# A mixture-of-experts stage on one Trainium2 core: fetching an expert's rows two experts ahead, with six-column one-hot products

## The chip, the cores and the metric

The kernel runs on one core of one Trainium2 chip. The metric is device time in microseconds (us) of one execution, lower is better. PE is the matrix engine TensorE, PEld its weight loads, DVE the VectorE, ACT the ScalarE, POOL the GpSimd engine, which issues indirect DMAs (gathers and scatters), and SP the engine that issues the weight loads from HBM. SBUF is the on-chip memory, PSUM the accumulator that PE writes.

## What is computed

The reference is one layer of a diffusion backbone for 512 tokens of width 1024: modulation from a conditioning vector, a mixer (RWKV-7 heads beside Fourier heads), a gated residual with layer norm, a second modulation, then a mixture of 32 experts and a last gated residual with layer norm. The part that matters here is the mixture:

- A router picks for each token 4 of 32 experts and gives softmax gates over the four.
- An expert is `y = W2 · swiglu(W1 · x + b1) + b2` with W1 of 1024 x 2048 and W2 of 1024 x 1024 in float32; `swiglu(g, l) = min(g, 7) · sigmoid(1.702 · min(g, 7)) · (clip(l, -7, 7) + 1)`.
- A token's result is the sum over its four experts of gate times y.

All 32 experts' weights, 12 MB each, are read once.

## The kernel before

The mixer and the router take the first part of the span; the expert stage begins at about 705 us, and a last layer norm closes the kernel.

**Capacities.** The experts are sorted by load and each place in a fixed list `PLAN` has a capacity of 32 to 192 rows, taken up as blocks of 64 or 32 rows: 53 blocks for the 32 places e0 to e31. (A loop for experts that overflow their capacity is in the program, and isn't executed.)

**Fetch.** `Expert.fetch` finds the tokens of an expert and gathers their rows. For a block, `slots` compares each token's rank in the expert with a row of numbers (one DVE instruction, `O`, a one-hot matrix of 512 tokens x 128 slots in bf16) and multiplies it on PE with a narrow right side `R6`: three columns give the row's index in parts (`onehot`, line 1249, 16 matmuls in 128 x 32 tiles, four of them side by side in the array). DVE makes the index `idx` of it (lines 1265 to 1269), and POOL issues the gather `xg` (line 1303). A second `onehot` over three other columns gives the gates, summed on DVE into `gt` (line 1275), which is needed only when the expert's result is scaled.

**Split, up, turn, down, put.** `split` transposes the gathered rows on PE (line 1314) and ACT copies them to `xt` (1316). `up` multiplies by W1 in 8 slices; each slice is one DMA of 1 MB into a `raw` tile (line 1326, on SP), used by the matmuls `st<-raw,xt` (line 1335) of every block, with the bias added at the end (1342) and swiglu on DVE and ACT (1369 to 1373). `turn` transposes the activations (1387, copy `at` on ACT 1389). `down` multiplies by W2 in four 1 MB tiles (`st<-raw,at`, also line 1335) and DVE scales by the gate into `y` (1406). `put` adds `y` to the rows of `accd` in HBM by an accumulating scatter (POOL, line 1412); these scatters follow one another, each waits for the landing of the one before. Four products `b2_part` (1477, `yb` 1478) add the gated b2 in the early experts.

**Order.** `all_experts` writes the stage as: for expert i, fetch of i+1, up of i, turn of i-1, split of i+1, down of i-1, put of i-1. The 384 weight loads go round 14 `raw` buffers, in program order on SP. [...] Buffers: two PSUM tiles `pt` for one-hot products and transposes, six for `st`; four gathered blocks `xg64` and two `xg32`; three `sel` (a column that adds the right expert's bias).

Of the kernel before, what the change touches and what calls it, by code (L numbers as in the profile page):

```python
# [1136 lines left out]
def _plan():  # L1137

    of = {n: [j for j in range(1, NE) if CAPS[j] == n] for n in (32, 64, 96)}
    plan = [0, of[32].pop()]  # L1140
    for j, rest in zip((3, 1, 4, 2, 5, 6), ((32, 96, 64, 96), (32, 64, 96, 64), (32, 96, 64, 96), (32, 64, 96, 64),
                                            (32, 96, 64, 96), (64, 96, 64, 32))):
        plan += [j] + [of[n].pop() for n in rest]
    return [(j, CAPS[j]) for j in plan]


PLAN = _plan()


def blocks(cap):  # L1150

    return [(o, min(64, cap - o)) for o in range(0, cap, 64)]
# [35 lines left out]
def moe(tc, I, ck, h2d, accd, modd, P):  # L1188
# [56 lines left out]
    def onehot(p, O, rhs, c):  # L1245
        for j in range(4):
            for i in range(4):
                q = slice(32 * i, 32 * i + 32)
                PE.matmul(p[q, c], O[:, j, q], rhs[:, j, c], start=(j == 0), stop=(j == 3), tile_position=(0, 32 * i))  # L1249

    def slots(cap, r, rhs):


        res = []
        ps = pst.tile([128, 512], F32, name="pt", tag="pt")
        for o, n in blocks(cap):
            w = 128 // n
            O = B.tile([128, 4, 128], BF16, "O", 5)
            io = M["iota"][:, o:o + n].unsqueeze(1).unsqueeze(1).to_broadcast([128, 4, w, n])
            V.tensor_tensor(O.rearrange("p j (a s) -> p j a s", s=n), io,  # L1260
                            r.unsqueeze(2).unsqueeze(2).to_broadcast([128, 4, w, n]), op=ALU.is_equal)
            p = ps[:, o // 8:o // 8 + 6]
            onehot(p, O, rhs, slice(0, 3))
            s3 = B.tile([128, 3], F32, "s3", 6)
            V.tensor_copy(s3, p[:, 0:3])  # L1265
            V.scalar_tensor_tensor(s3[:, 0:1], s3[:, 2:3], M[f"trash{n}"], s3[:, 0:1], op0=ALU.mult, op1=ALU.add)
            V.tensor_tensor(s3[:, 0:1], s3[:, 0:1], s3[:, 1:2], op=ALU.add)
            idx = B.tile([128, 1], I32, "idx", 10)
            V.tensor_scalar(idx, s3[:, 0:1], float(w), M[f"base{n}"], op0=ALU.mult, op1=ALU.add)  # L1269
            gt = B.tile([128, 1], F32, "gt", 10)  # L1270
            res.append((idx, gt, O, p))
        yield [z[0:2] for z in res]
        for _, gt, O, p in res:
            onehot(p, O, rhs, slice(3, 6))
            V.tensor_reduce(gt, p[:, 3:6], mybir.AxisListType.X, ALU.add)

    def part(i, n):
# [3 lines left out]
    class Expert:  # L1281
# [10 lines left out]
            return self  # L1292

        def fetch(self):
            more = slots(self.cap, self.r, self.rhs)
            self.sl = next(more)
            sel = B.tile([96, 64], BF16, "sel", 3)
            G.tensor_copy(sel, self.selcol.to_broadcast([96, 64]))  # L1298
            self.sel.append(sel)
            self.xs = []  # L1300
            for (idx, _), n in zip(self.sl, self.bl):
                x = B.tile([128, 8 * n], F32, f"xg{n}", n // 16)
                G.indirect_dma_start(out=x, out_offset=None, in_=h2h[n],  # L1303
                                     in_offset=bass.IndirectOffsetOnAxis(ap=idx[:, 0:1], axis=0))
                self.xs.append(x)
            for _ in more:
                pass
# [156 lines left out]
    def place(i):  # L1464
        j, cap = PLAN[i]
        return Expert(cap, rm[:, :, j], R6[:, :, j], sel3[:, j:j + 1])

    def chosen(i):
        j = PLAN[i][0]
        return SY.value_load(eidi[0:1, j:j + 1], min_val=0, max_val=NE - 1)  # L1470

    def b2_part(j):

        y = B.tile([128, D], F32, "yb", 1)
        for n in range(2):
            p = pst.tile([128, 512], F32, name="pt", tag="pt")
            PE.matmul(p, gwT[:, j * 128:(j + 1) * 128], b2r[:, n * 512:(n + 1) * 512], start=True, stop=True)
            A.activation(y[:, n * 512:(n + 1) * 512], p, AF.Copy)
        G.indirect_dma_start(out=accd[:, :], out_offset=bass.IndirectOffsetOnAxis(ap=toki[:, j:j + 1], axis=0),
                             in_=y, in_offset=None, compute_op=ALU.add)  # L1480

    def all_experts():
        cur, prev = first, None
        yield cur.split
        for i in range(len(PLAN)):
            nxt = place(i + 1) if i + 1 < len(PLAN) else None
            if nxt:
                yield nxt.fetch
            ups = list(cur.up())
            yield from ups[:8 if nxt else 4]  # L1490
            if nxt:
                nxt.weights(chosen(i + 1))
            if prev:
                yield prev.turn
            if nxt:
                yield nxt.split
            if prev:
                yield from prev.down()
                yield prev.put
                if 4 <= i < 8:  # L1500
                    yield lambda j=i - 4: b2_part(j)
            if not nxt:
                yield from ups[4:]
            prev, cur = cur, nxt
        yield prev.turn
        yield from prev.down()
        yield prev.put
# [14 lines left out]
    B = Buffers(None, 99, (praw, RAWA))  # L1522
    first = Expert(PLAN[0][1], rm0, R60, M["sel0"][0:96]).weights(0)
    experts = Run(all_experts())
    experts.load(RAWA)
    sb_ = ExitStack()
# [24 lines left out]
    for j in P.order:  # L1551
        tk = slice(j * 128, (j + 1) * 128)
        p = mixer(j)
# [200 lines left out]
    with ExitStack() as sv:  # L1754
# [3 lines left out]
        with tc.For_i(0, nov, 1) as k:  # L1758
# [8 lines left out]
            r, gq = pv.tile([128, 4], F32, name="ovr"), pv.tile([128, 4], F32, name="ovg")  # L1767
# [3 lines left out]
            rhs = pv.tile([128, 4, 6], BF16, name="ovrhs")  # L1771
# [68 lines left out]
```

## Time and profile before

| | before |
|---|---|
| median of 3 runs | 1832.53 us (1828.89 to 1835.13) |
| the profiled execution: its own time / span | 1826.18 us / 1824.4 us |
| mean granted TensorE clock, as a share of full speed | 0.934 |
| PE busy | 1627.3 us (89%) |
| PE weight loads busy | 890.5 us (49%) |
| DVE busy | 766.7 us (42%) |
| ACT busy | 390.4 us (21%) |
| POOL busy | 433.0 us (24%) |
| DMA | 572.83 MB, mean 314 GB/s |

The span is what the profiler records of one execution from its first to its last instruction; the run's own time is 1.8 us more. A row of a timeline gives start, length, engine, line and shapes (a float32 matmul instruction leaves two records in it); brackets at its end give the time that the engine sat idle just before, and what ended it. `SPq` is SP's own queue, and a wait of it for PE at line 1326 is a weight load that waits for a `raw` buffer to come free.

### The profile page before, as it was taken

What the parts mean: (1) busy time and instruction counts of PE and PEld (TensorE: products, weight loads), DVE (VectorE), ACT (ScalarE), POOL (GpSimd) and SP (SyncE); (2) the same over time, 40 slices, a digit from 0 to 9 for tenths busy, and PEclk for the clock granted to TensorE, in tenths of its full rate; (3) what the DMA queues carried; (4) which work ended last, traced back from release to release, by engine and by line L of the source; (5) the groups of instructions that cost most, each with busy time, mean ns of one, the idle gap of its engine ahead of it and who ended that gap; (6) DMA issues with size and microseconds to landing.
All of it is one profiled execution on the core that took longest, in us unless ns stands there. A gap on an engine that the chain in (4) does not pass through costs nothing. (4 is left out here: it accounts for less than half of the span.)

```text
span 1824.4 us, 40583 instructions
## 1 busy us (share of the span) xinstructions
PE 1627.3 (89%) x16964; PEld 890.5 (49%) x16964; DVE 766.7 (42%) x1775; ACT 390.4 (21%) x767; POOL 433.0 (24%) x436
## 2 busy tenths in 40 slices
PE   4889887686999977999989999999999999999980
PEld 1767655566787763454334443444344344434430
DVE  4899967878446673221122121222022221212113
ACT  3565455232224250100011000100010100001001
POOL 1543444264134351111120211011011110111113
PEclk9899988786899977999999999999999999999995
DMA  8568759574675638989997999999999999999993
GB/s 318 173 202 258 243 186 280 167 219 142 179 238 186 211 128 332 379 317 408 403 395 248 390 407 405 415 406 415 396 351 404 411 407 409 412 409 410 404 385 113
DMA packets 205514, 572.83 MB, mean 314 GB/s; under 512 B 28448, under 2 KB 116128, under 8 KB 156176
## 3 DMA queue, kind: packets, MB, share of 16 engines
q1 hardware_dynamic: 144912, 521.16, 73.9%
q0 software_dynamic: 11840, 24.91, 5.9%
q10 hardware_dynamic: 48576, 24.12, 4.7%
q8 instruction: 136, 2.23, 0.5%
q14 instruction: 50, 0.41, 0.1%
HBM read 512.57 MB, written 57.56 MB: 313 GB/s over the span
## 5 line engine op out<-in xcount | busy, mean ns | idle before, releaser
L1335 PE MATMUL st<-raw,xt 128*32 128x512 f32 (+1 forms) x6784 | 644.7, 521 | 5.9 <-ACT xt L1316 5.2
L1335 PEld LDWEIGHTS st<-raw,xt 128*32 128x32 f32 x6784 | 249.4, 109 | 329.4 <-issue 269.1
L1335 PE MATMUL st<-raw,at 128*32 128x512 f32 (+1 forms) x3392 | 324.4, 521 | 10.5 <-ACT at L1389 7.6
L1335 PEld LDWEIGHTS st<-raw,at 128*32 128x32 f32 x3392 | 115.2, 110 | 190.8 <-issue 148.4
L1369 DVE TENSOR_SCALAR sg<-st 128x256 f32<-128x256 f32 x87 | 36.4, 418 | 366.3 <-PE st L1342 366.3
L1370 ACT ACTIVATE sth<-sg 128x256 f32<-128x256 f32 x87 | 35.9, 415 | 572.2 <-DVE sg L1369 572.1
L1412 POOL DMA_INDIRECT accd<-y,idx x53 | 84.7, 1597 | 247.5 <-DVE y L1406 119.9
L1406 DVE SCALAR_TENSOR_TENSOR y<-st,gt,gt2h 128x512 f32<-128x512 f32 (+1 forms) x53 | 34.6, 654 | 236.8 <-PE st L1335 214.6
L1303 POOL DMA_INDIRECT xg<-h2d,idx x53 | 54.2, 1022 | 316.1 <-DVE idx L1269 295.8
L328 PE MATMUL pj<-hhi,wl 128*128 128x512 f32 (+1 forms) x240 | 89.9, 376 | 9.6 <-DVE wl L324 9.6
L328 PE MATMUL pj<-hhi,wh 128*128 128x512 f32 (+1 forms) x240 | 88.7, 372 | 9.8 <-DVE hlo L281 9.8
L1298 POOL CAST sel<-sel 96x64 bf16<-96x64 f32 x31 | 7.8, 254 | 361.6 <-PE st L1342 356.2
L328 PE MATMUL pj<-hlo,wh 128*128 128x512 f32 (+1 forms) x240 | 89.7, 374 | 0.0
L1316 ACT ACTIVATE xt<-pt 128x512 f32<-128x512 f32 (+1 forms) x53 | 27.3, 518 | 268.8 <-PE pt L1314 268.6
L652 PE MATMUL big<-Rb,Lt 128*128 128x256 f32 (+1 forms) x192 | 53.3, 428 | 14.9 <-DVE pk L658 6.4
L1265 DVE COPY s<-pt 128x3 f32<-128x3 f32 x53 | 8.3, 156 | 133.2 <-PE pt L1249 133.2
L1249 PEld LDWEIGHTS <-O 128*32 128x32 bf16 x1696 | 38.4, 95 | 51.6 <-issue 43.2
L328 PEld LDWEIGHTS pj<-hhi,wl 128*128 128x128 f32 x240 | 46.8, 195 | 21.6 <-DVE wl L324 12.4
L328 PEld LDWEIGHTS pj<-hhi,wh 128*128 128x128 f32 x240 | 46.8, 195 | 19.2 <-DVE hlo L281 10.1
L1389 ACT ACTIVATE at<-pt 128x512 f32<-128x512 f32 (+1 forms) x53 | 26.5, 517 | 132.1 <-PE pt L1387 131.8
L752 POOL TENSOR_TENSOR SW<-S,Wc 64x128 f32<-64x128 f32 (+1 forms) x66 | 31.3, 474 | 96.2 <-DVE S L787 77.5
L407 DVE SCALAR_TENSOR_TENSOR acc<-war,sil,acc 128x512 f32<-128x512 f32 x56 | 52.8, 943 | 0.8 <-ACT acc L404 0.6
(389 smaller groups left out, 2342.7 us busy)
## 6 DMA issues: line engine op xcount, KB each, us to landing
raw<-in_w SPq DMA_DIRECT2D x384, 1024.0 KB, 17.0
war<-in_w_ada SPq DMA_DIRECT2D x64, 256.0 KB, 3.3
chd<-pk ACTq DMA_DIRECT2D x52, 256.0 KB, 5.3
wr<-in_w_in ACTq DMA_DIRECT2D x40, 256.0 KB, 5.7
wa<-in_w_ada SPq DMA_DIRECT2D x16, 512.0 KB, 8.0
win<-chd SPq DMA_DIRECT2D x8, 896.0 KB, 5.6
win<-chd SPq DMA_DIRECT2D x16, 448.0 KB, 3.4
ltd<-Lt SPq DMA_DIRECT2D x8, 768.0 KB, 6.2
```

Of the source, the lines that this page charges most:

```text
L328: PE.matmul(p, a[:, k, :], b[:, k0 + k, t0:t0 + n], start=(k0 + k == 0 and i == 0), stop=(k0 + k == KD - 1 and i == 2))
L407: V.scalar_tensor_tensor(acc, wr, sil0[:, k:k + 1], acc, op0=ALU.mult, op1=ALU.add)
L652: PE.matmul(ps[:, z], Lu[:, u0 + (z0 + z if d == 0 else 3 - z0 - z), :], Rb[:, z0 + z], start=True, stop=True)
L752: G.tensor_tensor(SW[HALF[p]].rearrange("p z d c -> p (z d) c"), S[HALF[p], :, :, p].rearrange("p z d c -> p (z d) c"), Wc[HALF[p], 2 * c0 ...
L1249: PE.matmul(p[q, c], O[:, j, q], rhs[:, j, c], start=(j == 0), stop=(j == 3), tile_position=(0, 32 * i))
L1303: G.indirect_dma_start(out=x, out_offset=None, in_=h2h[n], in_offset=bass.IndirectOffsetOnAxis(ap=idx[:, 0:1], axis=0))
L1316: A.activation(xt.rearrange("p k s -> p (k s)"), p, AF.Copy)
L1335: PE.matmul(r, x(s * slices + b, o), c(raw[:, b * 2048 // slices:(b + 1) * 2048 // slices]), start=(s + b == 0 and first), stop=(s == n - ...
L1369: V.tensor_scalar(g, u2[:, :, 0], 7.0, None, op0=ALU.min)
L1370: A.activation(t, g, AF.Tanh, scale=0.851)
L1406: V.scalar_tensor_tensor(y, st, gt, gt2h[n], op0=ALU.mult, op1=ALU.mult)
L1412: G.indirect_dma_start(out=acch[n], out_offset=bass.IndirectOffsetOnAxis(ap=idx[:, 0:1], axis=0), in_=y, in_offset=None, compute_op=ALU.add)
```

## The change

It has two parts. `slots` gets an argument `once`: for every expert but the first, one group of 16 one-hot matmuls per block computes six columns, index and gates, instead of a group of three columns for the index and later one of three for the gates. And `all_experts` calls fetch two experts ahead: before up of i it fetches i+2 (and i=1 before the loop), where it fetched i+1.

```diff
-    def slots(cap, r, rhs):
+    def slots(cap, r, rhs, once):
...
-            onehot(p, O, rhs, slice(0, 3))
+            onehot(p, O, rhs, slice(0, 6 if once else 3))
...
         for _, gt, O, p in res:
-            onehot(p, O, rhs, slice(3, 6))
+            if not once:
+                onehot(p, O, rhs, slice(3, 6))
             V.tensor_reduce(gt, p[:, 3:6], mybir.AxisListType.X, ALU.add)
...
-            more = slots(self.cap, self.r, self.rhs)
+            more = slots(self.cap, self.r, self.rhs, self is not first)
...
         cur, prev = first, None
+        ahead = [place(i) for i in range(1, len(PLAN))]
         yield cur.split
+        yield ahead[0].fetch
         for i in range(len(PLAN)):
-            nxt = place(i + 1) if i + 1 < len(PLAN) else None
-            if nxt:
-                yield nxt.fetch
+            nxt = ahead[i] if i + 1 < len(PLAN) else None
+            if i + 2 < len(PLAN):
+                yield ahead[i + 1].fetch
```

Lines below it move by one or two: 1335 becomes 1337, 1303 becomes 1305, 1412 becomes 1414. Since the scheduler orders the instructions, the two programs were laid side by side, engine by engine. Over the expert stage 103 groups of 16 one-hot matmuls become 54, and 46 of them that stood at a place where the stream of `st` matmuls was not at a multiple of four become 17. Up to the bias of e17, the second expert with three blocks of 64 rows, 66 groups become 35, of which 30 and 12 are off that beat. Transposes `turn` that are followed directly by the `st` matmuls that need their copy go from 19 to 11 (up to there about half of them), and `split` so followed from 11 to 7. SP's order is the same in both.

On PE, at the block of 32 rows of an early expert (`R_5426` holds the columns, `at` belongs to the down pass that ends there, `xt` to the up pass that begins), the rows stand so; each LDWEIGHTS and MATMUL pair at line 1249 is repeated 16 times for a group. Before:

```order
L1335 MATMUL st<-raw,at_8054 32x256 x32
L1249 LDWEIGHTS O
L1249 MATMUL pt<-R_5426,O 32x3
...
L1335 MATMUL st<-raw,xt_8059 32x256 x19
L1249 LDWEIGHTS O
L1249 MATMUL pt<-R_5426,O 32x3
```

After:

```order
L1337 MATMUL st<-raw,at_8033 32x256 x32
L1249 LDWEIGHTS O
L1249 MATMUL pt<-R_5426,O 32x6
...
L1337 MATMUL st<-raw,xt_8038 32x256 x64
```

Before, groups of the fetch that ran beside this pass cut it after 19, 36 and 52 of its 64 matmuls; after, the 64 matmuls of the pass stand together.

On PE in the up pass of e17 (three blocks of 64 rows, `xt_12880`, `xt_12887`, `xt_12894` before and `xt_12431`, `xt_12438`, `xt_12445` after; `xg` with a transpose is the third block's split), eight matmuls per slice and block. Before:

```order
L1335 MATMUL st<-raw,xt_12880 32x512 x16
L1335 MATMUL st<-raw,xt_12887 32x512 x16
L1335 MATMUL st<-raw,xt_12880 32x512 x8
L1314 MATMUL pt<-mcst,xg_12616 128x128 x4
...
L1335 MATMUL st<-raw,xt_12894 32x512 x24
```

After (the first two blocks have gone through all eight slices by the rows ahead of these):

```order
L1337 MATMUL st<-raw,xt_12431 32x512 x8
L1337 MATMUL st<-raw,xt_12438 32x512 x8
...
L1344 MATMUL st<-b1s,sel 32x512
L1316 MATMUL pt<-mcst,xg_11963 128x128 x4
...
L1337 MATMUL st<-raw,xt_12445 32x512 x64
```

The third block's split moved from inside the pass to behind it, so its eight slices are used after the other two blocks are done with all of theirs.

On POOL at the end of the stage (each `accd` is a scatter, each `xg` a gather, `xg_17328` and `xg_16271` are those of the last expert). Before:

```order
L1412 DMA accd<-y_16322,idx 1280x512
L1303 DMA xg_17024<-h2d,idx 128x512
L1412 DMA accd<-y_16674,idx 1280x512
L1303 DMA xg_17328<-h2d,idx 128x256
L1412 DMA accd<-y_16676,idx 2560x256
L1412 DMA accd<-y_16988,idx 1280x512
L1412 DMA accd<-y_16990,idx 1280x512
L1412 DMA accd<-y_17295,idx 1280x512
L1412 DMA accd<-y_17544,idx 1280x512
L1412 DMA accd<-y_17546,idx 2560x256
L1412 DMA accd<-y_17627,idx 1280x512
L1412 DMA accd<-y_17717,idx 2560x256
```

After:

```order
L1414 DMA accd<-y_15981,idx 1280x512
L1305 DMA xg_16017<-h2d,idx 128x512
L1414 DMA accd<-y_15983,idx 2560x256
L1300 CAST sel<-sel_5427 96x64
L1414 DMA accd<-y_16235,idx 1280x512
L1305 DMA xg_16271<-h2d,idx 128x256
L1414 DMA accd<-y_16237,idx 1280x512
L1414 DMA accd<-y_16526,idx 1280x512
L1414 DMA accd<-y_16728,idx 1280x512
L1414 DMA accd<-y_16730,idx 2560x256
L1414 DMA accd<-y_16811,idx 1280x512
L1414 DMA accd<-y_16901,idx 2560x256
```

The last gather stands ahead of six scatters instead of eight, and its one-hot products stand one expert earlier on PE (in up of e29 instead of up of e30).

## Rows read from the trace of the kernel before

**Rows 1.** Windows of 20 us: time, busy time of each engine, clock, DMA.
```profile
core 0: us, PE busy (x) PEld busy (x) DVE busy (x) ACT busy (x) POOL busy (x), PEclk, DMA share, GB/s
920.00:940.00 20.00, 14.92 (x208) 6.33 (x206) 9.19 (x31) 3.90 (x8) 6.39 (x6) 0.91 1.03 401
...
980.00:1000.00 20.00, 19.53 (x211) 9.01 (x204) 9.04 (x26) 3.62 (x9) 0.26 (x2) 1.00 0.57 200
...
1300.00:1320.00 20.00, 20.00 (x192) 5.91 (x188) 0.00 (x0) 0.00 (x0) 1.57 (x1) 1.00 0.98 384
1320.00:1340.00 20.00, 19.53 (x266) 9.44 (x262) 9.98 (x30) 3.62 (x9) 3.89 (x4) 1.00 0.82 285
...
1420.00:1440.00 20.00, 20.00 (x252) 8.03 (x252) 5.01 (x19) 1.31 (x3) 4.77 (x5) 1.00 1.02 411
```

**Rows 2.** Waits of PE from 690 to 1800 us: total, times, longest.
```profile
PE st L1335 <- ACT at L1389: 7.6, 16, 0.7
PE st L1335 <- ACT xt L1316: 5.2, 10, 0.7
PE pt L1314 <- DMA xg<-h2d,idx: 4.6, 2, 3.7
...
PE st L1335 <- SPq L1758: 2.8, 2, 2.5
```

**Rows 3.** Waits of SP's queue from 800 to 1780 us.
```profile
SPq L1326 <- PE st L1335: 394.8, 195, 13.7
```

**Rows 4.** DMA issues of the page: count, size, median us from issue to landing.
```profile
raw<-in_w SPq DMA_DIRECT2D x384, 1024.0 KB, 17.0
```

**Rows 5.** Timeline of PE in up of e30: start, length, shapes, records.
```profile
1725.97 3.62 PE L1335 MATMUL st<-raw,xt 128*32 128x512 f32 x32
1729.41 0.26 PE L1249 MATMUL pt<-R,O 128*32 128x3 bf16 x16
1729.52 10.49 PE L1335 MATMUL st<-raw,xt 128*32 128x512 f32 x96
1739.82 0.62 PE L1342 MATMUL st<-b1s,sel 96*32 96x512 bf16 x8
```

**Rows 6.** Timeline of PE at a group that cuts the stream off the beat.
```profile
1222.19 3.18 PE L1335 MATMUL st<-raw,xt 128*32 128x512 f32 x27
...
1225.20 0.60 PE L1335 MATMUL st<-raw,xt 128*32 128x512 f32 x3
...
1225.68 0.60 PE L1335 MATMUL st<-raw,xt 128*32 128x512 f32 x1
...
1225.73 3.61 PE L1335 MATMUL st<-raw,xt 128*32 128x512 f32 x31
1229.12 0.26 PE L1249 MATMUL pt<-R,O 128*32 128x3 bf16 x11
```

**Rows 7.** Timeline of POOL's gathers and scatters at the end, some of them.
```profile
1727.91 0.99 POOL L1303 DMA_INDIRECT xg<-h2d,idx  x1 [28.97 <-DVE idx L1269]
1729.20 1.59 POOL L1412 DMA_INDIRECT accd<-y,idx  x1 [0.30 <-issue]
1738.90 1.57 POOL L1412 DMA_INDIRECT accd<-y,idx  x1 [8.11 <-DMA accd<-y,idx]
...
1791.11 1.55 POOL L1412 DMA_INDIRECT accd<-y,idx  x1 [3.74 <-issue]
```

**Rows 8.** Timeline of DVE, the scaled results of the last experts.
```profile
1726.12 0.75 DVE L1406 SCALAR_TENSOR_TENSOR y<-st,gt,gt2h 128x512 f32<-128x512 f32 x1 [4.64 <-PE pt L1249]
1752.01 1.34 DVE L1406 SCALAR_TENSOR_TENSOR y<-st,gt,gt2h 128x512 f32<-128x512 f32 x2 [8.71 <-PE st L1335]
1770.89 0.74 DVE L1406 SCALAR_TENSOR_TENSOR y<-st,gt,gt2h 128x512 f32<-128x512 f32 x1
1781.13 0.48 DVE L1406 SCALAR_TENSOR_TENSOR y<-st,gt,gt2h 128x256 f32<-128x256 f32 x1 [9.50 <-PE st L1335]
```

**Rows 9.** The chain that ended last, the piece behind the last scatter's issue.
```profile
1791.11 3.78 DMA accd<-y,idx
```

## The prediction

> **What bounds the kernel now.** I read the windows of 20 us first. In the expert stage PE is busy nearly all the time (19.5 to 20.0 of 20 us) at full clock, and at the same time the DMA engines are full: a share of 1.02 at 411 GB/s in the window at 1420 [rows 1], and so in nearly all windows of the stage. The places where transfers fall off are few: 200 GB/s at 980, 384 at 1300, 285 at 1320 [rows 1]; behind 1340 there is none up to 1760. So two limits lie side by side, and the list of waits has to say which ends last. PE waits little over 1100 us: 7.6 us in 16 waits for the copy `at`, 5.2 us in 10 for the copy `xt`, and 2.8 us for weights, nearly all of it once at the very end [rows 2]. SP's loads wait 394.8 us for PE to free a `raw` buffer [rows 3]. From this I take PE as the pace up to about 1340, with some weights landed ahead of it; from there the transfers run without a gap, the lead is used up, and at the end PE waits for the last tiles. What PE saves before 1340 can therefore move the end, and what it saves behind it cannot. After the weights comes a second chain: POOL's scatters, each behind the landing of the one before. The last `y` is ready at 1781.13 + 0.48 = 1781.6 [rows 8], yet its scatter is issued at 1791.11 [rows 7] and lands 3.78 us later [rows 9]; only then the layer norm starts. These 9.5 us are a queue on POOL.
>
> **The change part by part.**
>
> *One-hot groups.* A group that stands on the beat of the `st` stream: 96 records of 128 x 512 took from 1729.52 to 1739.82, 0.107 us each. The 32 records ahead of it need 3.43 us, and from 1725.97 to 1729.52 there are 3.55 [rows 5]: the group costs 0.12 us of PE. A group that cuts it: from 1222.19 to 1229.12 are 6.93 us with 62 `st` records, 6.65 us of work [rows 6], so 0.28 us; I take 0.30. The price of a group with six columns isn't in the trace. Three columns cost 0.12 us beside 512, so the weights and the issue rather than the columns set it; the bounds are 0.12 (columns free) and 0.24 (double), and I take 0.12, since a group's 0.12 us for 16 matmuls is next to one record of 512 columns (0.107). By the counts of the order, before the bias of e17 (at about 1325 us) 36 x 0.12 + 30 x 0.30 = 13.3 us become 23 x 0.12 + 12 x 0.30 = 6.4: -6.9 us. Behind it, 21 x 0.12 + 16 x 0.30 = 7.3 become 14 x 0.12 + 5 x 0.30 = 3.2: -4.1 us. With 0.24 for six columns, 23 x 0.12 and 14 x 0.12 come back, 2.8 and 1.7 us.
>
> The Trainium skill, "TensorE: Matmul & The Clock Gate", section "Back-to-back issue gap", gives matmuls of 1 to 64 columns one floor of about 25 ns each, whatever their width. That agrees with six columns costing as three; but 16 of them would be an estimated 0.40 us, where rows 5 show 0.12, since four of them stand side by side in the array. By the page the groups would be worth 49 x 0.40 = 19.6 us in all instead of 11.0; the row decides.
>
> *Waits on copies.* Where `turn` or `split` stands right before the product that needs its copy, PE waits 7.6 / 16 = 0.48 and 5.2 / 10 = 0.52 us [rows 2]. The order has 8 and 4 fewer such places: -3.8 - 2.1 = -5.9 us, about half of it, -3.0, before e17.
>
> So PE's own work is shorter by 6.9 + 3.0 = 9.9 us up to e17 and by 7.0 behind it. The 7.0 are hidden by the transfers, which have no gap there; without that cover they would count in full.
>
> *The third block of e17.* A new cost. Its eight `raw` tiles were freed one by one, each after three blocks. Now they are first freed after two blocks have gone through all eight: 128 instructions, 256 records of 0.107, 27.4 us in which none of eight of the 14 buffers comes free. What is under way then covers a load's median time from issue to landing, 17.0 us [rows 4]. So transfers rest for some 10.4 us. Before, there was a rest at the same place: (411 - 384) / 411 x 20 = 1.3 and (411 - 285) / 411 x 20 = 6.1 us [rows 1], 7.4 in all. The net is +3.0 us; bounds are +10.4 (the old rest was no part of it and stays) and 0. The second block of e27 is put off in the same way, by 13.7 us, less than the 17.0 under way: 0. All of this is late in being refilled, not in being used, so PE itself needn't wait there.
>
> PE's end: -9.9 + 3.0 = -6.9, taken as -7; bounds -17 (all of PE's saving counts, no new rest) and +0.5 (10.4 new, all of 9.9 saved).
>
> *The tail.* In up of e30, POOL waits 28.97 us for the last gather's index, while finished results stand behind it: the gather goes at 1727.91 and then eight scatters at steps of about 9.8 us (1729.20, 1738.90) [rows 7], though a `y` of them was ready long before. After, that gather stands one expert earlier, ahead of six scatters; its products stand in up of e29, which begins before 1700. Then the scatters can go as their `y` comes: 1726.9, 1752.8, 1762.6, 1772.4, and the last at 1782.2 by four steps of 9.8 from 1752.8 at the latest, next to 1781.6. In place of 1791.1 that is -9; bounds 0 and -9.5.
>
> *Others.* The same number of gathers, scatters, DVE index steps and loads is left; `gt` is now ready earlier, and its `tensor_reduce` is not on a path. Fetching earlier holds gathered rows and `idx` longer; PE waited for gathered rows only at the start of the stage, 4.6 us [rows 2], which the change doesn't touch (the first expert keeps its two groups). So the fetch itself buys nothing but the order.
>
> *Sum.* -7 - 9 = -16 us. The profiled execution's own 1826.2 becomes 1810.2; the median of before is 6.3 above it, and by the same difference I predict 1832.5 - 16 = **1816.5**.
>
> **The rivals.** About 0.3% (5.5 us) is what a measurement of this kernel can tell from no change.
>
> A, both terms as above: 1816.5, with its own range 1805 to 1820. Chance 0.45.
>
> B, the transfers bind before 1340 too, and PE's saving only makes it wait: for it speaks the full share in nearly every window [rows 1]; against it, that PE waits for no weights before the end [rows 2]. Then only the tail counts, and the e17 rest in part: -9, 1823.5. Chance 0.20.
>
> C, the tail is no shorter, because scatters pile up behind another gather or behind each other's landing; for it, that six steps of 9.8 us fill 59 of the last 90 us. PE's -7 is left: 1825.5. Chance 0.12.
>
> D, slower: the e17 hold hits when no tile is landed ahead. PE then stands for 10.4 us, and for some 2 more the clock is low, as in the window at 920, where 5 us of idle time went with a granted 0.91 over 20 us, below full speed for 0.09 x 20 = 1.8 us [rows 1]. With the transfers as the bound, PE's savings before it don't count, and PE comes to the tail that much later, with its scatters still in a row: +12.2 us, less the 7.4 of rest that transfers had at this place before if these were lost then too. That is 1837 to 1845. It decides from the point where PE shows a wait for `raw` of over 7 us between 1300 and 1345. Chance 0.10.
>
> The Trainium skill, same page, section "Loop structure matters more than you think", warns of just this: matmuls that wait for DMA run at the low clock afterwards. The window at 920, with 5 us idle and 0.91, agrees that idle time and a low clock come together here.
>
> E, no change that can be measured: one-hot products stood in PE's shadow of the weights anyway and the scheduler's order gives as it takes: 1832.5 within 5.5. For it, PE never waited for a gather but at the start. Chance 0.13.
>
> **How the numbers follow.** Faster is A, B and C: 0.77; the same 0.13, slower 0.10. The range reaches from 1804, a bit beyond A's bound with half of PE's hidden saving, to 1831, which takes in B and C and half of E, and leaves out D, the other half of E and some 0.04 below.
>
> **What would show it.** PE's line 1249 should fall to about half its instructions, the waits for `at` and `xt` to some 11 and 7 times. In the windows from 1300 to 1360 the transfers should dip deeper than before, with hardly a PE wait for `raw`. The last scatter should be issued within 1.5 us of the last `y`, and that `y` 7 us earlier than 1781.6. It is wrong if PE's idle time for `raw` moves from the end into the stage, if the last `y` is not earlier, or if scatters still stand in a row of 9.8 us steps up to the end.

## The result, and the profile after

The changed kernel takes 1815.23 us (median of 5 runs, 1809.78 to 1816.04) against 1832.53 us (1828.89 to 1837.62, 5 runs) measured beside it: a ratio of 0.9901 with a 95% interval of 0.9887 to 0.9916, so about 17 us less. Beside a ratio, here and below, a gain in us is the difference of two medians. Two more comparisons gave 0.9906 (0.9880 to 0.9933) and 0.9901 (0.9882 to 0.9920). The profiled execution took 1809.78 us with a span of 1808.0, 16.4 us less than the span before.

The tail first: POOL's last gather and the scatters behind it, and from DVE's timeline the last `y`.

```profile
1683.87 1.02 POOL L1305 DMA_INDIRECT xg<-h2d,idx  x1 [0.31 <-issue]
1691.77 1.57 POOL L1414 DMA_INDIRECT accd<-y,idx  x1 [6.88 <-DMA accd<-y,idx]
1712.47 1.56 POOL L1414 DMA_INDIRECT accd<-y,idx  x1 [19.13 <-DVE y L1408]
...
1758.52 1.55 POOL L1414 DMA_INDIRECT accd<-y,idx  x1 [7.51 <-issue]
1774.63 1.55 POOL L1414 DMA_INDIRECT accd<-y,idx  x1 [14.55 <-DVE y L1408]
```

```profile
1773.87 0.48 DVE L1408 SCALAR_TENSOR_TENSOR y<-st,gt,gt2h 128x256 f32<-128x256 f32 x1 [9.13 <-PE st L1337]
```

The releaser of the last scatter is now `y`, where before scatters stood in a row behind each other's landing [rows 7]. It is issued 0.3 us after the last `y` is ready (1774.35), where it was 9.5 us. And that `y` itself comes 7.3 us earlier than the 1781.6 of before [rows 8]. These two are the 16.5 us by which the last scatter moved.

Next PE's waits in the changed kernel, in two stretches: 690 to 1560 us, and 1560 to 1800 us.

```profile
PE st L1337 <- ACT xt L1318: 3.9, 2, 3.5
PE st L1337 <- DMA raw<-in_w: 2.0, 4, 0.6
```

```profile
PE st L1337 <- DMA raw<-in_w: 12.0, 15, 1.8
PE st L1337 <- SPq L1762: 3.1, 3, 1.4
```

Before, PE waited 0.7 us for `raw` tiles beside the 2.8 us of [rows 2], and all of it behind 1560; over 690 to 1800 us:

```profile
PE st L1335 <- DMA raw<-in_w: 0.7, 1, 0.7
```

Now it waits for weights again and again, but late: 12.0 + 3.1 = 15.1 us lie behind 1560, where it was 3.5. What PE saved there has become waiting, as the prediction had it. Over the whole stretch the wait for `at` fell from 16 times to 7 (3.1 us) and that for `xt` from 10 to 5 (6.0 us, of which 3.5 in one piece at e17, which was not foreseen).

A second wait was not foreseen either. Over 690 to 1800 us PE now stands twice for `yb`, the copy of a `b2_part` product, where it stood once (before, then after), and the new wait is at 950 (a row of PE, then one of ACT):

```profile
PE pt L1249 <- ACT yb L1478: 3.3, 1, 3.3
PE pt L1249 <- ACT yb L1480: 6.5, 2, 3.3
```

```profile
949.94 0.26 PE L1249 MATMUL pt<-R,O 128*32 128x6 bf16 x16 [3.15 <-ACT yb L1480]
949.29 1.09 ACT L1480 ACTIVATE yb<-pt 128x512 f32<-128x512 f32 x2 [20.34 <-DMA accd<-yb,toki]
```

In the new order, which the tile framework's scheduler makes when the program is built, a one-hot group stands on PE behind a `b2_part` product; that product keeps its `pt` tile until ACT can copy it into the one `yb` buffer, which the scatter of the `yb` before still holds. All eight traces of kernels that fetch two experts ahead at this place have this second wait, of 1.7 to 4.0 us, and none of the six others has it.

The windows around e17, with the columns of [rows 1]:

```profile
1280.00:1300.00 20.00, 16.46 (x176) 5.30 (x172) 6.32 (x21) 2.15 (x5) 2.48 (x2) 0.99 0.83 346
1300.00:1320.00 20.00, 19.53 (x172) 6.35 (x168) 3.79 (x12) 1.93 (x5) 5.75 (x5) 0.92 0.94 341
1320.00:1340.00 20.00, 19.79 (x302) 11.92 (x297) 5.50 (x18) 1.99 (x4) 5.46 (x5) 1.00 1.03 393
...
1420.00:1440.00 20.00, 20.00 (x247) 8.07 (x250) 6.29 (x22) 3.28 (x7) 3.10 (x4) 1.00 1.02 408
```

The rest of the transfers moved from 1320 to 1280, and PE stands for 3.5 us there, behind which the granted clock of a window is 0.92. The timeline of PE shows why:

```profile
1265.65 27.77 PE L1337 MATMUL st<-raw,xt 128*32 128x512 f32 x256 [0.40 <-DMA raw<-in_w]
1293.24 1.05 PE L1344 MATMUL st<-b1s,sel 96*32 96x512 bf16 x16
1294.22 0.66 PE L1316 MATMUL pt<-mcst,xg 128*128 128x128 f32 x4
1294.80 0.26 PE L1249 MATMUL pt<-R,O 128*32 128x6 bf16 x16
1298.60 15.64 PE L1337 MATMUL st<-raw,xt 128*32 128x512 f32 x128 [3.54 <-ACT xt L1318]
```

Two blocks take 27.8 us over all eight tiles (27.4 forecast), then the third block is transposed, PE waits for the copy, and the tiles come free only from 1298.6. The copy came late because it stood on ACT behind the swiglu of these two blocks, whose steps wait for DVE:

```profile
1294.80 0.42 ACT L1372 ACTIVATE sth<-sg 128x256 f32<-128x256 f32 x1 [0.24 <-DVE sg L1371]
1296.47 0.42 ACT L1372 ACTIVATE sth<-sg 128x256 f32<-128x256 f32 x1 [1.25 <-DVE sg L1371]
1297.65 0.42 ACT L1372 ACTIVATE sth<-sg 128x256 f32<-128x256 f32 x1 [0.76 <-DVE sg L1371]
1297.97 0.58 ACT L1318 ACTIVATE xt<-pt 128x512 f32<-128x512 f32 x1
```

Nor was this block fetched earlier. On DVE its index had been one instruction short since 1216, and came behind the swiglu of the pass ahead:

```profile
1216.23 0.16 DVE L1268 TENSOR_TENSOR s<-s 128x1 f32<-128x1 f32 x1
...
1261.40 0.21 DVE L1270 TENSOR_SCALAR idx<-s,mcst 128x1 int32<-128x1 f32 x1
```

Its gather, the 32nd of 53, went at 1261.88, where before the 32nd went at 1259.4. PE's transposes at 1294.22 didn't wait for it, so the late index is not what cost the 3.5 us.

Last, the price of a group with six columns, on the beat, from PE's timeline:

```profile
1404.45 5.76 PE L1337 MATMUL st<-raw,at 128*32 128x512 f32 x52
1410.03 0.26 PE L1249 MATMUL pt<-R,O 128*32 128x6 bf16 x16
1410.13 6.20 PE L1337 MATMUL st<-raw,xt 128*32 128x512 f32 x56
```

52 records of 0.1073 us (10.30 us for 96 of them in rows 5) end at 1410.03, and the next pass begins at 1410.13: 0.10 us. Six columns cost no more than three did (0.12, rows 5); the upper bound of 0.24 is out.

### The profile page after: what moved, and what is told of

Same layout as the page of the kernel before. It is cut to its first block, busy times and chain, and to the rows that moved or that the text cites. A ratio compares the mean times of both kernels' runs of the same rounds, so it can differ in the third digit from the quotient of the medians.

```text
span 1808.0 us, 38957 instructions
## 1 busy us (share of the span) xinstructions
PE 1609.5 (89%) x16148; PEld 873.1 (48%) x16148; DVE 760.8 (42%) x1775; ACT 390.5 (22%) x767; POOL 435.7 (24%) x436
## 5 line engine op out<-in xcount | busy, mean ns | idle before, releaser
L1337 PE MATMUL st<-raw,xt 128*32 128x512 f32 (+1 forms) x6784 | 631.9, 523 | 19.2 <-DMA raw<-in_w 11.9
L1337 PEld LDWEIGHTS st<-raw,xt 128*32 128x32 f32 x6784 | 243.0, 110 | 368.4 <-issue 283.8
L1337 PE MATMUL st<-raw,at 128*32 128x512 f32 (+1 forms) x3392 | 318.9, 520 | 7.4 <-ACT at L1391 3.1
L1337 PEld LDWEIGHTS st<-raw,at 128*32 128x32 f32 x3392 | 110.1, 110 | 188.8 <-issue 148.3
L328 PEld LDWEIGHTS pj<-hlo,wh 128*128 128x128 f32 x240 | 47.0, 196 | 12.9 <-issue 6.4
L652 PEld LDWEIGHTS big<-Rb,Lt 128*128 128x128 f32 x192 | 38.8, 239 | 21.1 <-issue 11.1
```

What stands on the lines that cost most here:

```text
L328: PE.matmul(p, a[:, k, :], b[:, k0 + k, t0:t0 + n], start=(k0 + k == 0 and i == 0), stop=(k0 + k == KD - 1 and i == 2))
L652: PE.matmul(ps[:, z], Lu[:, u0 + (z0 + z if d == 0 else 3 - z0 - z), :], Rb[:, z0 + z], start=True, stop=True)
L1337: PE.matmul(r, x(s * slices + b, o), c(raw[:, b * 2048 // slices:(b + 1) * 2048 // slices]), start=(s + b == 0 and first), stop=(s == n - ...
```

## The experiments

Twelve runs in four groups, each group on one chip with runs of before beside it. Diffs are against the changed kernel, but for the last fetch alone, which is against before. The table counts, from the packets of each trace, when the weight loads landed (load 0 to 383; 200 to 207 are those of e17's up pass), as the time between two landings; behind it the end of the last `y`, how long the last scatter was issued after it, and the medians of the timed runs with those of before in the same group. The first group is six columns alone (first trace), early fetch alone, six columns up to e17, and from e18; none of its runs of before was traced. Stages are compared by differences, since the stage itself starts at slightly different times (load 32 landed at 766.9 to 775.8 us).

| kernel | 32 to 200 | 200 to 224 | 224 to 383 | 32 to 383 | last `y` | scatter behind it | median us / before |
|---|---|---|---|---|---|---|---|
| before, 2 traces | 497.1, 496.8 | 71.4, 71.5 | 437.1, 437.1 | 1005.7, 1005.4 | 1781.6, 1782.9 | 9.5, 9.7 | |
| changed, 3 traces | 488.9, 490.3, 490.1 | 73.6, 75.3, 72.6 | 436.8, 437.3, 437.5 | 999.3, 1002.9, 1000.3 | 1774.3, 1780.6, 1778.0 | 0.3, 0.3, 0.3 | 1815.2/1832.5, 1812.5/1829.1, 1815.4/1831.9 |
| six columns alone, 2 traces | 494.7, 492.5 | 69.1, 68.8 | 437.4, 437.9 | 1001.2, 999.2 | 1777.3, 1775.4 | 6.1, 6.1 | 1818.6/1835.4, 1818.2/1831.9 |
| early fetch alone | 497.1 | 68.8 | 442.5 | 1008.5 | 1783.9 | 0.3 | 1822.4/1835.4 |
| six columns up to e17 | 490.9 | 76.3 | 437.4 | 1004.5 | 1782.1 | 0.3 | 1816.4/1835.4 |
| six columns from e18 | 498.8 | 68.7 | 442.6 | 1010.0 | 1787.8 | 0.3 | 1821.5/1835.4 |
| last fetch alone | 497.5 | 71.0 | 438.5 | 1007.0 | 1783.0 | 1.4 | 1821.0/1829.1 |
| six columns, last fetch | 493.8 | 68.8 | 438.1 | 1000.8 | 1777.8 | 1.8 | 1815.0/1829.1 |
| e16 to e18 late, 2 traces | 489.8, 489.6 | 67.6, 67.7 | 438.3, 438.7 | 995.7, 996.0 | 1772.8, 1766.2 | 0.3, 0.3 | 1811.2/1831.9, 1809.0/1827.6 |

**Six columns alone.**

```diff
         yield cur.split
-        yield ahead[0].fetch
...
-            if i + 2 < len(PLAN):
-                yield ahead[i + 1].fetch
+            if nxt:
+                yield nxt.fetch
```

> One group of six columns per block, but fetch one expert ahead as before. PE saves by the counts of the order 7.2 us before the bias of e17 and 5.0 behind it; the last gather still stands ahead of eight scatters. My theory (only what PE saves before e17 moves the end, and the tail needs the earlier fetch): -7 us against before, 1825.5, with the last scatter some 9 us behind the last result. Rival 1 (all that PE saves counts): -12, 1820. Rival 2 (transfers bind everywhere, PE's saving is worth nothing): 0, 1832.5.

The median came to 0.9914 of before (0.9896 to 0.9932), 16.8 us, twice what I expected and level with the whole change. The trace shows less: weights 4.5 us sooner, and the last scatter 6.1 us behind the last `y` in place of 9.5. That is 8; on this gap see below.

**Early fetch alone.**

```diff
-            more = slots(self.cap, self.r, self.rhs, self is not first)
+            more = slots(self.cap, self.r, self.rhs, False)
```

> Fetch two experts ahead, but two groups of three columns per block. The third block of e17 is put off as in the changed kernel. PE saves 2.8 us before e17 and 2.0 behind it. My theory: the tail gives -9, PE's end about 0 to +1 (2.8 saved, the rest of the transfers at e17 given back), so 1823.5. Rival 1 (the six columns give it all, the early fetch nothing): 1832.5. Rival 2 (every saving counts and e17 costs nothing): -14, 1818.5.

0.9932 (0.9915 to 0.9949), 12.9 us. The tail is as forecast, 0.3 us. The weights take 3 us longer than before, not the same. Nothing of PE's saving shows up to load 200: this kernel too has the second wait for `yb`, 3.81 us at 951. The place where it loses is not e17 (68.8 us) but loads 260 to 383, with a window that shows a rest of the transfers where before there was none:

```profile
1460.00:1480.00 20.00, 20.00 (x292) 9.29 (x288) 2.72 (x11) 0.38 (x1) 0.98 (x1) 1.00 0.85 346
```

In the order of this kernel the tiles of e22's up pass, loads 260 on, are held for an estimated 28 us (262 records of 0.107), as those of e17 are. The order of the changed kernel has no such hold there.

At e17 this trace says something on the changed kernel. The third block is put off here as well:

```profile
1276.40 25.93 PE L1337 MATMUL st<-raw,xt 128*32 128x512 f32 x238
1302.25 0.66 PE L1316 MATMUL pt<-mcst,xg 128*128 128x128 f32 x4
1302.95 1.89 PE L1337 MATMUL st<-raw,xt 128*32 128x512 f32 x16
```

The tiles are held for 26 us, yet loads 200 to 224 take 68.8 us, less than before. PE doesn't stand for the copy here. The four traces with that wait of 3.54 us take 72.6 to 76.3 us at this place, the ten without it 67.6 to 71.5. So at this place it is the hold together with the wait that costs, and not the hold alone.

**Six columns up to e17, and from e18 on.**

```diff
-            more = slots(self.cap, self.r, self.rhs, self is not first)
+            more = slots(self.cap, self.r, self.rhs, self is not first and self.early)
```

`early` is set for the places up to e17; in the second kernel the condition is `not self.early`, so that e0 and the places up to e17 have two groups.

> The changed kernel, but from e18 on the two groups of three columns are back. PE's work before e17 is as in the changed kernel, behind it 2.6 us longer. My theory: what PE saves behind e17 is hidden by the transfers, so the time is that of the changed kernel, 1815.2 within 1.5 us. Rival (all that PE saves counts): +2.6 to +3.1 us, 1818.

> The changed kernel, but up to e17 the two groups of three columns are back; one group of six from e18 on. PE's work before e17 is 7.9 us longer than in the changed kernel, behind it the same. My theory: the time goes back by most of that, to 1822 or 1823, that of the kernel with the early fetch alone. Rival (transfers bind everywhere): 1815 as in the changed kernel. Rival (all savings count alike): 1822 too, told apart by the run with six columns up to e17.

0.9894 (0.9873 to 0.9915) with the six columns early, and 0.9927 (0.9909 to 0.9944) with them late. The first is level with the changed kernel: the groups behind e17 are worth nothing, and loads 224 to 383 take 437.4 us with them and without. The second gave back some 3 us of the 17 by the medians, 4 to 5 by the ratios; I had expected 7. In its trace the stage up to load 200 has lost the whole gain (498.8 us). It doesn't isolate that loss, though: its order has no wait for the copy at e17 (68.7 us), and loads 224 to 383 take 5 us more, with a hold at e22 as in the kernel with the early fetch alone (256 records in 27.65 us from 1448). Against that kernel its six columns from e18 on brought nothing (442.6 and 442.5 us).

**Before, and the changed kernel, again.** Both unchanged.

> The kernel before, unchanged, for a second trace: the traced execution was 6.3 us under the median of its runs. If the 16.8 us that six columns alone brought are to be found in the traces, then this trace, if near the median (1832 to 1836), shows its last weights landing 5 to 8 us later than the first trace's 1778.7, or its tail that much longer. If the first trace was a fair one, the stage ends as there.

> The changed kernel, unchanged, beside the others of this call: 1815 to 1818. If both parts had effects that add, as my sum had it, six columns alone could not reach 1818.6 and the early fetch alone 1822.4; so the expectation is that the two parts save the same microseconds and this stays within 4 us of the first.

The second trace of before (1828.07 us, in a group with a median of 1829.1) repeats the first in every stage within 1 us, so the first was a fair one. The second trace of the changed kernel has its last `y` only 1 to 2 us earlier than before; the tail's 9.3 us are there again.

**Only the last fetch earlier.**

```diff
         cur, prev = first, None
+        ahead = [place(i) for i in range(1, len(PLAN))]
...
-            nxt = place(i + 1) if i + 1 < len(PLAN) else None
-            if nxt:
+            nxt = ahead[i] if i + 1 < len(PLAN) else None
+            if nxt and i < len(PLAN) - 2:
                 yield nxt.fetch
+            if i == len(PLAN) - 3:
+                yield ahead[-1].fetch
```

> The kernel before, with only the last expert's fetch one expert earlier; the other fetches, and all groups of three columns, as before. PE's order is the same but for the last two experts. Theory of the tail (the last gather's index holds POOL while results stand behind it): -9 us against before, with the last scatter within 1.5 us of the last result. Rival (the scatters are late for another reason, each other's landing): 0 to -3, with scatters in a row of steps of some 10 us up to the end.

0.9952 (0.9933 to 0.9970), 8.1 us, with nothing else touched. POOL's timeline of this kernel:

```profile
1700.02 0.95 POOL L1303 DMA_INDIRECT xg<-h2d,idx  x1 [2.15 <-DVE idx L1269]
1701.28 1.62 POOL L1412 DMA_INDIRECT accd<-y,idx  x1 [0.31 <-issue]
...
1776.01 1.56 POOL L1412 DMA_INDIRECT accd<-y,idx  x1 [10.04 <-DVE y L1406]
1784.49 1.55 POOL L1412 DMA_INDIRECT accd<-y,idx  x1 [6.92 <-DMA accd<-y,idx]
```

The gather that held POOL until 1727.91 is out at 1700.02, and the last scatter follows the last `y` by 1.4 us, while the weights land no sooner (438.5 us for loads 224 to 383 where before has 437.1, last `y` at 1783.0).

**Six columns and only the last fetch earlier.** The two edits above together.

> Six columns, fetch one expert ahead, and only the last expert's fetch one expert earlier: the saving on PE without the third block of e17 put off, and the tail. If tail and PE add, 1818.6 less the 6.2 us between the last result and its scatter that the run with six columns alone shows: 1813. If they don't, 1818.

0.9924 (0.9899 to 0.9949), 14.1 us: in the trace the two effects do add up (weights 1000.8, scatter 1.8 us behind), yet it is no better than six columns alone by the ratios, whose intervals overlap. It doesn't beat the changed kernel. Beside the kernel with the last fetch alone, in the same group, it is the plainest test of PE's saving: the two differ in the six columns (and the order that comes of them), and the weights take 6.2 us less, 3.7 of them up to load 200 and 2.2 up to load 224, and the median is 6.0 us lower.

**Six columns alone, and the changed kernel, side by side.**

> Six columns, fetch one expert ahead, once more beside before and the changed kernel. Its first run's median stood 16.8 us under before, while its trace against the two traces of before accounts for 3.4 to 4.9 us of weights and 3.5 us of tail, 7 to 8. If the traces are right: -8 against before and 6 to 8 us behind the changed kernel. If the medians are: -16, level with the changed kernel.

> The changed kernel, unchanged, for the comparison within this call, and a third trace: -16 to -17 against before; from load 200 to load 224 it takes 73.6 to 75.2 us, where six columns alone take 69.

0.9926 (0.9910 to 0.9943) and 0.9901 (0.9882 to 0.9920): 13.7 and 16.5 us. For six columns this is less than the first run's 16.8 and more than the 8 to 10 us that the traces account for. The scatters of six columns alone, at the last gather and at the end:

```profile
1715.19 0.98 POOL L1305 DMA_INDIRECT xg<-h2d,idx  x1 [29.41 <-DVE idx L1270]
1716.48 1.59 POOL L1414 DMA_INDIRECT accd<-y,idx  x1 [0.30 <-issue]
...
1781.55 1.55 POOL L1414 DMA_INDIRECT accd<-y,idx  x1 [4.25 <-issue]
```

The gather still waits 29 us for its index, but is out 12.7 us sooner than before, so a third of the tail is gone without an earlier fetch.

**e16 to e18 fetched one expert ahead.**

```diff
-            if i + 2 < len(PLAN):
+            if i + 1 in (16, 17, 18):
+                yield nxt.fetch
+            if i + 2 < len(PLAN) and i + 2 not in (16, 17, 18):
                 yield ahead[i + 1].fetch
```

> The changed kernel, but e16, e17 and e18 are fetched one expert ahead as before. By the order the weight tiles of e17 are held 20.6 us for five of the eight and 13.7 for one, where the changed kernel holds them 17 to 29 us. Theory (the hold at e17 gives back some of PE's saving): loads 200 to 224 in 70 to 72 us in place of 74, and 2 to 4 us faster than the changed kernel. Rival (the rest at this place is the stage's own, whoever holds the tiles): the same as the changed kernel within 1.5 us.

> The changed kernel with e16 to e18 fetched one expert ahead, once more, since its six runs went from 1805 to 1822 and its interval overlaps that of the changed kernel. If the hold at e17 costs what the trace showed (loads 200 to 224 in 67.6 us in place of 72.6 to 75.3), the ratio to before is again at or under 0.989, and the second trace has 67 to 70 us there. If the first trace was luck, the ratio is 0.990 to 0.991 and the place takes 72 us or more.

0.9892 (0.9862 to 0.9921) and 0.9896 (0.9874 to 0.9918). The traces are clear: 67.6 and 67.7 us for loads 200 to 224, and 996 us in all where the changed kernel has 999 to 1003. In PE's timeline of the first, the third block is no longer put off:

```profile
1287.66 0.66 PE L1316 MATMUL pt<-mcst,xg 128*128 128x128 f32 x4
...
1291.90 22.49 PE L1337 MATMUL st<-raw,xt 128*32 128x512 f32 x208
1314.22 1.47 PE L1344 MATMUL st<-b1s,sel 96*32 96x512 bf16 x24
```

and the windows there show no 3.5 us of idle time:

```profile
1280.00:1300.00 20.00, 20.00 (x218) 5.95 (x212) 2.66 (x12) 0.60 (x1) 3.56 (x3) 1.00 1.02 406
1300.00:1320.00 20.00, 19.53 (x192) 6.20 (x186) 5.33 (x16) 2.79 (x7) 3.44 (x3) 1.00 1.00 394
```

The ratios are lower than the changed kernel's three by 0.0005 to 0.0014, well inside their intervals. It beats before; that it beats the changed kernel is likely from the traces, and not shown by the times.

## Why the prediction was right

Its number, 1816.5, was 1.3 us from the median, and case A, both terms, is what happened. That it came so near is in part luck: in the traces some terms came out too large, and one had the right size from a wrong picture. Term by term:

- **The tail, -9.** Shown. The last scatter's lag fell from 9.5 and 9.7 to 0.3 us, a gain of 9.2 to 9.4, and the edit that moves only the last gather brought 8.1 us. Rival C is out. (The working has a slip: from 1752.8 to 1782.2 are three steps of 9.8, not four.)
- **PE's saving up to e17, -9.9.** Right in kind, too large. Loads 32 to 200 take 497 us before and 489 to 490 after: -6.7 to -8.1. The second wait for `yb`, 3.15, 2.16 and 1.95 us in the three traces, has the size of what is missing; the prediction had put such effects of the earlier fetch at nothing ("buys nothing but the order"). No run takes that wait away by itself. That the saving moves the end, and doesn't only make PE wait, is shown by the six columns beside the last fetch, 6 us in time and weights alike: rival B is out. The prediction's list of rests left out two that lie in this stretch (268 and 341 GB/s from 780 to 820, 263 at 960); the sum doesn't change by them.
- **The third block of e17, +3.0.** Loads 200 to 224 went from 71.4 to 72.6, 73.6 and 75.3: +1.2 to +3.9. The size is right by luck, its picture is not. The transfers do not rest longer in bytes (by the prediction's reckoning, (411 - 346) / 411 x 20 + (411 - 341) / 411 x 20 = 6.6 us, against 7.4 before), and "PE itself needn't wait there" was wrong: it stands 3.5 us for the copy of the late block. Where the third block is put off too and that wait is missing, the place takes 68.7 and 68.8 us. Taking the early fetch away for e16 to e18 alone removes the cost and a few microseconds more.
- **PE's saving behind e17, hidden.** Shown: with its groups of six or with two groups of three, loads 224 to 383 take 437 us, and PE's waits for weights behind 1560 rise from 3.5 to 15.1 us.
- **PE's end, -7.** The stage is 2.5 to 6.4 us shorter in the three traces, -4.7 on average. With the tail that is -14 in the traces where the sum had -16, and the three medians say -16.5 to -17.3. In the traces the sum was 2 us too large, in the medians 1 too small.

What stays open is this difference of some 3 us between traces and medians. It is not the same everywhere: against the two traces of before it is 7 to 9 us for the four kernels of the first group, where before had its highest median (1835.4) and no trace, and 0 to 5 us for all others. The two traces of before lie 1.0 and 6.3 us under the medians of their own groups, and the runs of before in one group spread over 7 to 13 us, so chance in which execution was traced can make much of it. A slower stretch of before that these traces don't hold, and that the change shortens as well, isn't excluded; no run shows one.

The prediction's sum took the two parts as one. By the medians they don't add: 13 us for the early fetch alone and 14 to 17 for the six columns alone make 17 together. By the traces they nearly do, 6 and 8 to 10 us against 14, so that much of the apparent overlap is the gap of the first group. Some overlap is plain: the tail has only 9.5 us to give, and six columns alone take 3.4 of them. And alone, the early fetch lengthens the stage by 3 us, through the wait for `yb` and a hold at e22 that the changed kernel's order doesn't have.

On the two rules of the Trainium skill: by "TensorE: Matmul & The Clock Gate", section "Back-to-back issue gap", width doesn't matter to matmuls of 1 to 64 columns, and the 0.10 us of six columns agrees; its floor of some 25 ns each does not fit 16 of them in 0.10 us side by side. By the section "Loop structure matters more than you think", waiting costs the clock; behind the 3.5 us at e17 the window's granted clock was 0.92, which agrees, but this wait was for a copy. The wait of 3.15 us at 950 left the windows from 940 to 980 at 1.00, and the PE waits for weights of up to 1.8 us each late in the stage left it at 1.00 in the windows from 1340 to 1760.

## What to carry to other kernels

Where the engine and the transfers are both full, mark the last window in which the transfers rest: what the engine saves ahead of it shortens the kernel, what it saves behind it becomes waiting. An in-order queue that mixes gathers and scatters makes finished results wait behind an index that isn't ready; look at the last entries of that queue first, since their lag lies on the end in full. And when a step is fetched earlier, look in the new order for what the matrix engine then meets that it didn't before: here a group that stands behind a product whose buffer isn't free (2 to 3 us), and a copy that stands behind other work (3.5 us, in a pass that gave back about a third of what had been gained ahead of it, 2.4 of 7.2 us on average). Buffers that are held longer cost by themselves where the transfers had no rest before (e22), and not where they had one (e17).

## What was not expected

The rate of loads in a full stretch hardly varies: 159 loads from 224 to 383 took 436.8 to 438.7 us in twelve of the fourteen traces, over seven programs with different orders on PE, 2.75 us a load with gathers and scatters between them. The two others are those of the kernels whose e22 held its tiles.
